# A decoder layer in split fp32: the down matrix's weight sums are made in the tail's second half instead of beside the main stage, and attention's line ends at 870

## The chip, the cores and the metric

The kernel runs on one core of one Trainium2 chip. A core has five engines with instruction streams of their own: PE (TensorE, matrix products), DVE (VectorE), ACT (ScalarE), POOL (GpSimd) and SP (SyncE, which issues most DMA transfers here). The metric is the device time of one execution in microseconds (us); the time of the kernel is the median of its runs.

## The reference

One trunk layer on 2048 tokens of 1024 channels, all in float32. It has a convolutional and an attention branch side by side, one output projection, and a gated feed-forward part of 2816 hidden channels:

```python
a = _rmsnorm(h, g_pre_mix[l])
u = jnp.einsum("bsd,dc->bsc", a, w_in[l])     # conv value | conv gate | q | k | v, 512 columns each
...
conv_out = _conformer_conv(c_val, c_gate, ...)   # GLU, causal depthwise conv of width 31, LayerNorm, silu
attn_out = _stick_breaking(q, k, v)              # 8 heads of 64; sigmoid(z) * prod of (1 - sigmoid) between
attn_out = _rmsnorm(attn_out, attn_norm_g[l]).reshape(B, S, SB_WIDTH)
y = jnp.einsum("bsc,cd->bsd", jnp.concatenate([conv_out, attn_out], axis=-1), w_out[l])
h = h + _rmsnorm(y, g_post_mix[l])
f_in = _rmsnorm(h, g_pre_ffn[l])
gt = jnp.einsum("bsd,df->bsf", f_in, w_gate[l])
up = jnp.einsum("bsd,df->bsf", f_in, w_up[l])
f = jnp.einsum("bsf,fd->bsd", jax.nn.silu(gt) * up, w_down[l])
h = h + _rmsnorm(f, g_post_ffn[l])
```

## The kernel before

**Products.** Each fp32 operand is split into a high part (`wH`, `xH`) that PE can take and a low rest (`wL`, `xL`); ACT makes the high part, POOL or DVE the rest. A product is three matrix products, low by high, high by high and high by low, on 128x512 tiles.

**The feed-forward part** uses a scheme of seven products instead of eight for each 2x2 block of matrices. It needs combinations of four quarters of the weights: per block `j` of `HF` = 11 and per matrix four sums for gate and up (88 in all, kept as `S`), and four for the down matrix (44, kept as `wd` with the numbers 5, 7, 6 and 4). `sums()` makes them on POOL from pieces of 128x512, which SP loads into three tiles called `sum`, and stores them in memory (L846 the sum, L840 the load, L768 the store).

**The main stage** walks the four groups of 512 tokens by a table, `PLAN`: the in-projection (PE writes `inps`), the two halves of the mixed output projection (`outc`, `outa`, PE writes `ops`), then products of the feed-forward part (`c11`, `p4`). The entries' costs add up to positions from 0 to 932. Beside it three generators are advanced: attention (`ATTN`), the taps of the convolution (`TAPS`, DVE, L476) and the weight sums (`SUMS`); each of the three tables says which share of its generator is due at which position. A unit of attention is: z on PE (L562, L563), sigmoids on ACT (L568, L570), a scan on DVE (`om`, L572), a product on POOL (`A`, L573), transposes on PE (`at`, L589), a split on ACT and DVE (`TH`, `TL`), and the value product `o` on PE (L594, L595). What is left of attention when the table's products are done is run alone, and then the last half of the output projection.

**The tail.** `five()` runs 44 blocks of gate and up, the first 22 for one half of the tokens and the last 22 for the other. A block is five products of twelve matrix products each (L762, PE writes `b`; four in the first half, where the fifth, `p4`, was made in the main stage). Its weights come from `S` through tiles `raw` (L1055, a DMA on SP); ACT and POOL split them (`wH` L1066, `wL` L1067). What a block adds up runs on DVE (L1074). Between the blocks a table `todo` calls other work, such as `input_sums`, which read sums of the inputs (`sumin<-B`, L815) into operands. The operands of products 6 and 5 of the first half lie in four large tiles under `x2` (`xH`, `xL`). After the first half these tiles are free until the down products, whose operands are split at L1254 to L1257 and whose products write `dps`.

**What sets the order.** Program order is a priority only: a scheduler places each engine's instructions by simulated time when the program is built. Instructions that go through `tc.keep_in_program_order` keep theirs.

Of the kernel before, what the change touches and what calls it, by code (L numbers as in the profile page):

```python
# [9 lines left out]
F32 = mybir.dt.float32  # L10
# [18 lines left out]
G = 512  # L29
# [36 lines left out]
    ("outc", 3, 22),  # L66
)

ATTN = ((46, 0.0), (890, 1.0))
TAPS = ((30, 0.0), (130, 0.168), (170, 0.25), (260, 0.418), (300, 0.5), (410, 0.668), (450, 0.75), (650, 0.918), (700, 1.0))  # L70
SUMS = ((330, 0.0), (900, 1.0))

# [66 lines left out]
def layer_kernel(ctx: ExitStack, tc: tile.TileContext, x, xT, g_pre_mix, w_in, conv_w, conv_b, ln_g, ln_b,  # L139
                 attn_g, w_out, g_post_mix, g_pre_ffn, w_gate, w_up, w_down, g_post_ffn, out):  # L140
    nc = tc.nc
# [88 lines left out]
    class Weights:  # L230
# [9 lines left out]
        def next(self):  # L240
            while len(self.tiles) < min(self.n + 1 + self.ahead, len(self.srcs)):
                self.tiles.append(self.load(self.srcs[len(self.tiles)]))
            self.n += 1
            return self.tiles[self.n - 1]
# [56 lines left out]
    for c in range(CB):  # L301
        t = vp.tile([P, PAD + G], F32, name=f"glu{c}")
# [160 lines left out]
    def taps(g):  # L463

        acc = vp.tile([P, CB, G], F32, tag="acc", name="acc", bufs=1)
        conv[g] = dp.tile([P, CB, G], F32, name=f"conv{g}")
        for c in range(CB):
            yield need(("val", g, c))
            a = pp.tile([P, G], F32, tag="cv", name="cv", bufs=1)
            tc.keep_in_program_order(  # L470
                nc.vector.tensor_scalar(a, gl[c][:, 0:G], cw[:, c, 0:1], cb_[:, c:c + 1], ALU.mult, ALU.add))
            yield 1
            for k in range(1, CW):
                to = acc[:, c, :] if k == CW - 1 else a
                tc.keep_in_program_order(
                    nc.vector.scalar_tensor_tensor(to, gl[c][:, k:k + G], cw[:, c, k:k + 1], a, ALU.mult, ALU.add))  # L476
                yield 1
            done.add(("taps", g, c))
        for _ in range(TAPLAG):
            yield 3  # L480
        yield from convnorm(g, acc)
# [265 lines left out]
    HF = NF // 2  # L747
    add, sub, mult = ALU.add, ALU.subtract, ALU.mult
# [5 lines left out]
    def four(t):  # L754
        return [t[:, i, :] for i in range(4)]
# [10 lines left out]
    def store(t, *key, eng=nc.sync):  # L766
        stored[key] = dp.tile([P, *t.shape[1:]], F32, name="_".join(str(k) for k in key))
        eng.dma_start(stored[key], t)  # L768

    def part(t, k, n, *key, eng=nc.sync):  # L770

        if key not in stored:
            stored[key] = dp.tile([P, n, G], F32, name="_".join(str(k) for k in key))
        eng.dma_start(stored[key][:, k, :], t)
# [61 lines left out]
    def sums():  # L836

        def piece(w, j, e):
            t = fup.tile([P, G], F32, tag="sum", name="sum", bufs=3)
            nc.sync.dma_start(t, w[j][:, e * G:(e + 1) * G])  # L840
            return t

        late = []

        def combine(c, a, b, op, *key):
            nc.gpsimd.tensor_tensor(c, a, b, op)  # L846
            late.append((c, *key))

        def flush(n):
            while len(late) > n:  # L850
                t, kind, *key, m = late.pop(0)
                if kind == "S":
                    ns = (6, 7) if m in (6, 7) else (5, 3)
                    part(t, ns.index(m), 2, kind, *key, ns)
                else:
                    store(t, kind, *key, m)

        for j in range(HF):
            for i, w in enumerate(W):
                a21, a22, a11 = piece(w, j + HF, 0), piece(w, j + HF, 1), piece(w, j, 0)  # L860
                yield 1
                combine(a22, a21, a22, add, "S", i, j, 5)
                yield 1
                combine(a21, a21, a11, sub, "S", i, j, 7)
                combine(a11, a22, a11, sub, "S", i, j, 6)
                yield 1
                flush(0)
                a12 = piece(w, j, 1)
                yield 1
                combine(a12, a12, a11, sub, "S", i, j, 3)  # L870
                yield 1
                flush(0)
        for j in range(HF):
            b12, b11, b22 = piece(w_down, j, 1), piece(w_down, j, 0), piece(w_down, j + HF, 1)
            yield 1
            combine(b11, b12, b11, sub, "wd", j, 5)
            yield 1
            combine(b12, b12, b22, sub, "wd", j, 7)
            combine(b22, b22, b11, sub, "wd", j, 6)
            yield 1  # L880
            flush(0)
            b21 = piece(w_down, j + HF, 0)
            yield 1
            combine(b21, b21, b22, sub, "wd", j, 4)
            yield 1
            flush(0)

    def input_sums(g, k, tmp, banks=bank, t4=None):

# [53 lines left out]
    def chain(gens):  # L943
        for gen in gens:
            yield from gen

    attn_s = Side(chain(attn(g) for g in range(NG)), 1 / (2 * NH * P * sum(16 * g + 10 for g in range(NG))), ("attn",))
    taps_s = Side(chain(taps(g) for g in range(NG)), 1 / (NG * (CB * CW + 3 * (TAPLAG + LAG * TT))), ("taps", "conv"))
    sums_s = Side(sums(), 1 / (15 * HF))
    fns = {"prep": (prep, 8), "qkv": (lambda g: inproj(g, qkv), 12), "gv": (lambda g: inproj(g, gv), 8),  # L950
           "in": (lambda g: inproj(g, both), 20),
           "mixc": (lambda g: mixed(g, 0), 1), "outc": (lambda g: outproj(g, 0), 4),
# [2 lines left out]
    def each(fn):  # L955
        def gen(g):
            for t in range(TT):
# [6 lines left out]
             "tprep": tprep}  # L964
    sides = ((attn_s, ATTN), (taps_s, TAPS), (sums_s, SUMS))
    pos = 0
    for name, g, cost, *mid in PLAN:
        fn, total = fns[name]
        pos += cost
        todo = []  # L970
# [11 lines left out]
        n = 0  # L982
# [15 lines left out]
    with ExitStack() as E:  # L998
# [6 lines left out]
        def operand(*slots, dt=F32R):  # L1005
            return [pool.tile([P, 4, G], dt, tag=tag, name=f"{tag}_", bufs=2 if pool is xp else 1)
                    for pool, tag in slots]

        e = [(ep, f"e{i}") for i in range(6)]
        x2 = [(xp, "xH"), (xp, "xL")]  # L1010
# [89 lines left out]
        late = []  # L1100

        def flush(n):
            for e in late:
                e[0] -= 1
            while n and late and late[0][0] < 0:
                store(*late.pop(0)[1:])
                n -= 1
# [4 lines left out]
        def five(early, todo):  # L1112
# [40 lines left out]
            for n in range(NB):  # L1153
                b3 = gu("b3")
                b.mul(b.b2, 7, False)
                nxt = Block(n + 1) if n + 1 < NB else None
# [41 lines left out]
                fn(*args)  # L1198
            next(more_h.pop())
            assert next(more, None) is None  # L1200
            for _ in range(9):
                flush(2)

        operands(0, [(6, x2), (5, x2), (7, e[4:6]), (3, e[0:2])])
        R = []
        last = NG - 2

        def steps():

# [18 lines left out]
        todo = {n: [(next, more)] * (1 if n < 5 else 2 - n % 2) for n in range(17)}  # L1228
        todo[17] = todo[18] = [(next, more)]
        todo[2 * HF - 1] = [(operands, last, [(3, e[0:2])], nc.gpsimd)]  # L1230
        five({2 * HF - 1: [(operands, last, [(7, e[4:6])])]}, todo)


# [164 lines left out]
```

## Time and profile before

| what | value |
|---|---|
| time, three runs | 2581.54, 2574.46, 2579.35 us; median 2579.35 |
| the profiled execution | 2579.23 us; its span 2577.5 us, mean granted clock 0.977 |
| PE | busy 2430.0 us, 94% of the span, 11156 instructions |
| POOL | busy 1482.5 us, 58% |
| DVE, ACT | busy 1793.3 us (70%), 1291.5 us (50%) |
| sums of weights, L846 | 132 of them, 171.8 us on POOL, 1302 ns each |
| the tail's two halves of gate and up | about 1557 to 1821 and 1821 to 2135 us |

The page first gives each engine's busy time. A busy engine that waits for nothing sets the pace; an idle stretch of it is what can be won. A row of waits names the engine and line that waited, the engine and line that it waited for, the total in us, how often, and the longest. In a timeline, a row gives start, duration, engine, line, operation and tiles, and in brackets the idle time before it with what ended it. In rows of the chain (the work that ended last, followed back) a row gives start, duration and what.

### The profile page before, as it was taken

What the parts mean: (1) busy time and instruction counts of PE and PEld (TensorE: products, weight loads), DVE (VectorE), ACT (ScalarE), POOL (GpSimd) and SP (SyncE); (2) the same over time, 40 slices, a digit from 0 to 9 for tenths busy, and PEclk for the clock granted to TensorE, in tenths of its full rate; (3) what the DMA queues carried; (4) which work ended last, traced back from release to release, by engine and by line L of the source; (5) the groups of instructions that cost most, each with busy time, mean ns of one, the idle gap of its engine ahead of it and who ended that gap; (6) DMA issues with size and microseconds to landing.
All of it is one profiled execution on the core that took longest, in us unless ns stands there. A gap on an engine that the chain in (4) does not pass through costs nothing.

```text
span 2577.5 us, 35682 instructions
## 1 busy us (share of the span) xinstructions
PE 2430.0 (94%) x11156; PEld 1963.3 (76%) x11156; DVE 1793.3 (70%) x2321; ACT 1291.5 (50%) x2398; POOL 1482.5 (58%) x1844
## 2 busy tenths in 40 slices
PE   7999989998999998999999979999999999998997
PEld 6878767776777776887788857777788878887886
DVE  5797689967997798887544547766655655557556
ACT  4455555655555655667666645332332233454543
POOL 5764668556755776639533228755443444567556
PEclk9999989998999899999999989999999999999999
DMA  9989877988898998857777746977656667668655
GB/s 360 303 301 311 287 244 260 369 262 272 273 328 287 314 329 285 275 189 230 263 257 243 242 140 235 340 265 234 213 189 201 199 200 266 195 189 286 204 188 171
DMA packets 289182, 657.32 MB, mean 255 GB/s; under 512 B 33888, under 2 KB 42080, under 8 KB 288992
## 3 DMA queue, kind: packets, MB, share of 16 engines
q1 hardware_dynamic: 264704, 622.01, 72.0%
q10 hardware_dynamic: 24288, 33.04, 3.5%
q8 instruction: 88, 1.44, 0.2%
q14 instruction: 102, 0.84, 0.1%
HBM read 460.92 MB, written 193.99 MB: 254 GB/s over the span
## 4 chain that ended last, share of the span: by engine, by line
PE 52%; DVE 11%; POOL 5%; DMA 4%; issue 3%; ACT 2%; SPq 0%; POOLq 0%; ACTq 0%; DVEq 0%
PE b L762 17%; PE dps L762 13%; PE c L762 8%; DVE cv L476 3%; DVE om L572 2%; PE at L589 2%; PE p L762 1%; PE ops L688 1%; PE ops L689 1%; PE ops L690 1%; PE o L595 1%; PE z L562 1%; PE o L594 1%; PE z L563 1%; DVE TL L249 1%
## 5 line engine op out<-in xcount | busy, mean ns | idle before, releaser
L573 POOL TENSOR_TENSOR A<-A,om 128x512 f32<-128x512 f32 (+2 forms) x320 | 313.7, 980 | 415.9 <-DVE om L572 364.3
L572 DVE TENSOR_TENSOR_SCAN om<-om,one,z 128x513 f32<-128x513 f32 (+2 forms) x320 | 351.3, 1112 | 114.5 <-ACT A L570 103.2
L1067 POOL TENSOR_TENSOR wL<-raw,wH 128x512 fp32r<-128x512 f32 x176 | 255.6, 1478 | 262.9 <-issue 164.6
L476 DVE SCALAR_TENSOR_TENSOR cv<-glu,cw,cv 128x512 f32<-128x512 f32 x464 | 346.6, 747 | 6.7
L1257 DVE TENSOR_TENSOR xL__22001<-t__22003,xH__22000 128x512 fp32r<-128x512 f32 x154 | 199.3, 1302 | 159.5 <-ACT xH__22000 L1256 159.3
L1255 POOL TENSOR_TENSOR xL__21999<-t__22002,xH__21998 128x512 fp32r<-128x512 f32 x154 | 207.8, 1354 | 173.3 <-ACT xH__21998 L1254 172.7
L256 PE MATMUL inps<-xH,wL 128*128 128x512 f32 x640 | 260.8, 408 | 12.9 <-ACT sg L422 11.0
L249 DVE TENSOR_TENSOR TL<-at,TH 128x512 fp32r<-128x512 f32 (+1 forms) x320 | 188.2, 598 | 110.3 <-ACT TH L248 109.8
L260 PE MATMUL inps<-xL,wH 128*128 128x512 f32 x640 | 258.4, 405 | 0.5 <-DVE xL L392 0.5
L258 PE MATMUL inps<-xH,wH 128*128 128x512 f32 x640 | 258.6, 405 | 0.0
L762 PE MATMUL dps<-xH__21998,xL__22001 128*128 128x512 f32 x616 | 240.9, 391 | 8.1 <-DVE xL__22001 L1257 7.2
L568 ACT ACTIVATE om<-z 128x512 f32<-128x512 f32 (+2 forms) x320 | 171.6, 539 | 153.0 <-DVE z L565 70.8
L762 PE MATMUL dps<-xL__21999,xH__22000 128*128 128x512 f32 x616 | 240.6, 391 | 2.2 <-POOL xL__21999 L1255 2.2
L762 PE MATMUL dps<-xH__21998,xH__22000 128*128 128x512 f32 x616 | 240.2, 390 | 0.0
L846 POOL TENSOR_TENSOR sum<-sum 128x512 f32<-128x512 f32 x132 | 171.8, 1302 | 89.3 <-DMA sum<-in_w_up_dram 33.4
L248 ACT ACTIVATE TH<-at 128x512 fp32r<-128x512 f32 (+1 forms) x320 | 168.2, 547 | 106.3 <-PE at L589 102.4
L1254 ACT ACTIVATE xH__21998<-t__22002 128x512 fp32r<-128x512 f32 x154 | 97.1, 631 | 231.9 <-POOL xL__21999 L1255 151.5
L589 PE MATMUL at<-idr,A 128*128 128x128 f32 x1088 | 192.1, 280 | 10.5 <-POOL A L573 9.3
L210 ACT ACTIVATE wH<-raw 128x1024 fp32r<-128x1024 f32 x156 | 165.8, 1065 | 53.5 <-DMA raw<-in_w_in_dram 19.1
L570 ACT ACTIVATE A<-z 128x512 f32<-128x512 f32 (+2 forms) x320 | 168.4, 542 | 21.0 <-PE at L589 13.6
L589 PEld LDWEIGHTS at<-idr,A 128*128 128x128 f32 x1088 | 142.0, 144 | 48.5 <-POOL A L573 12.4
L1066 ACT ACTIVATE wH<-raw 128x512 fp32r<-128x512 f32 x176 | 101.1, 623 | 154.8 <-PE b L762 77.1
(296 smaller groups left out, 6226.3 us busy)
## 6 DMA issues: line engine op xcount, KB each, us to landing
wL<-wL SPq DMA_DIRECT2D x156, 512.0 KB, 5.2
raw<-in_w_in_dram SPq DMA_DIRECT2D x80, 512.0 KB, 6.0
t__22003<-u SPq DMA_DIRECT2D x154, 256.0 KB, 2.8
c<-c ACTq DMA_DIRECT2D x88, 256.0 KB, 4.6
t__22002<-wd SPq DMA_DIRECT2D x88, 256.0 KB, 2.9
K<-kd SPq DMA_DIRECT2D x80, 256.0 KB, 4.6
V<-vd SPq DMA_DIRECT2D x80, 256.0 KB, 4.5
u<-accf SPq DMA_DIRECT2D x22, 768.0 KB, 4.2
```

Of the source, the lines that this page charges most:

```text
L249: nc.vector.tensor_tensor(L, ps, H.bitcast(F32), ALU.subtract)
L256: nc.tensor.matmul(ps, WL[:, kc], aH[t](k), start=k == 0, stop=False)
L258: nc.tensor.matmul(ps, WH[:, kc], aH[t](k), start=False, stop=False)
L260: nc.tensor.matmul(ps, WH[:, kc], aL[t](k), start=False, stop=k == KT - 1)
L476: nc.vector.scalar_tensor_tensor(to, gl[c][:, k:k + G], cw[:, c, k:k + 1], a, ALU.mult, ALU.add))
L572: nc.vector.tensor_tensor_scan(r, r, z[:, 0:1].to_broadcast([P, w + 1]), one, ALU.mult, ALU.bypass)
L573: nc.gpsimd.tensor_tensor(a[:, 0:w], a[:, 0:w], om[:, G - w + 1:G + 1], ALU.mult)
L589: nc.tensor.transpose(pt[:, j * P:(j + 1) * P], u["A"][j][:, b * P:(b + 1) * P], id32)
L762: return nc.tensor.matmul(ps, a, b, skip_group_check=True, **flags)
L1067: nc.gpsimd.tensor_tensor(l, t, f32(h), sub)
L1255: nc.gpsimd.tensor_tensor(WL, w, f32(WH), sub)
L1257: nc.vector.tensor_tensor(UL, t, f32(UH), sub)
```

## The change

The generator `sums()` loses the 44 sums of the down matrix, and its scale goes from 15 to 10 steps a block. A new generator `down_sums()` makes them in the tail: its pieces lie in the four tiles of `x2`, which give a ring of sixteen 128x512 pieces, four of which make up one `j`. Four pieces are loaded by SP at a time, the sums are made on POOL in place, pinned in program order, and stored through the queue `late`, from which each product of a block stores up to two entries. Blocks 22 to 43 each advance the generator twice, so two sums a block. The last flush at the end of the blocks takes twelve entries instead of nine. In the attention table, 890 becomes 870.

```diff
-ATTN = ((46, 0.0), (890, 1.0))
+ATTN = ((46, 0.0), (870, 1.0))
...
-        for j in range(HF):
-            b12, b11, b22 = piece(w_down, j, 1), piece(w_down, j, 0), piece(w_down, j + HF, 1)
-            yield 1
-            combine(b11, b12, b11, sub, "wd", j, 5)
-            yield 1
-            combine(b12, b12, b22, sub, "wd", j, 7)
-            combine(b22, b22, b11, sub, "wd", j, 6)
-            yield 1
-            flush(0)
-            b21 = piece(w_down, j + HF, 0)
-            yield 1
-            combine(b21, b21, b22, sub, "wd", j, 4)
-            yield 1
-            flush(0)
...
-    sums_s = Side(sums(), 1 / (15 * HF))
+    sums_s = Side(sums(), 1 / (10 * HF))
...
-            for _ in range(9):
+            next(more_wd)
+            for _ in range(12):
                 flush(2)
...
+        def down_sums():
+
+            wd = cycle([p for _ in range(2) for t in operand(*x2, dt=F32) for p in four(t)])
+
+            def piece(j, e, c):
+                t = next(wd)
+                nc.sync.dma_start(t, w_down[j][:, c * G:(c + 1) * G])
+                return t
+
+            def pinned(*args):
+                tc.keep_in_program_order(nc.gpsimd.tensor_tensor(*args))
+
+            def get(j):
+                return piece(j, 0, 1), piece(j, 0, 0), piece(j + HF, 0, 1), piece(j + HF, 0, 0)
+
+            nxt = get(0)
+            yield
+            for j in range(HF):
+                b12, b11, b22, b21 = nxt
+                pinned(b11, b12, b11, sub)
+                late.append([1, b11, "wd", j, 5])
+                yield
+                pinned(b12, b12, b22, sub)
+                late.append([1, b12, "wd", j, 7])
+                yield
+                pinned(b22, b22, b11, sub)
+                late.append([1, b22, "wd", j, 6])
+                yield
+                pinned(b21, b21, b22, sub)
+                late.append([1, b21, "wd", j, 4])
+                yield
+                if j + 1 < HF:
+                    nxt = get(j + 1)
...
+        more_wd = down_sums()
+        for n in range(2 * HF, 4 * HF):
+            todo[n] = todo.get(n, []) + [(next, more_wd)] * 2
```

The line numbers of the changed kernel are 14 lower between the two edits (L1067 becomes L1053, L1055 L1041), and 24 higher behind them (L1257 becomes L1281); the new load is L1201 and the new sum L1205.

Three places show how the instructions now stand. First POOL at the switch from the tail's first to its second half. `raw_19797` of before and `raw_19577` of after hold the same block's weights. Before:

```order
L1067 TENSOR_TENSOR wL<-raw_19698,wH 128x512 x2
L810 TENSOR_TENSOR e__19805<-sumin,e__19804 128x512 x4
L1067 TENSOR_TENSOR wL<-raw,wH 128x512 x2
L1067 TENSOR_TENSOR wL<-raw_19797,wH 128x512 x2
L1067 TENSOR_TENSOR wL<-raw,wH 128x512 x2
L1067 TENSOR_TENSOR wL<-raw_19924,wH 128x512 x2
```

After:

```order
L1053 TENSOR_TENSOR wL<-raw_19577,wH 128x512 x2
L1205 TENSOR_TENSOR xH__19708<-xH__19708 128x512
L1053 TENSOR_TENSOR wL<-raw,wH 128x512 x2
L1053 TENSOR_TENSOR wL<-raw_19704,wH 128x512 x2
L1205 TENSOR_TENSOR xH__19708<-xH__19708 128x512 x2
L1053 TENSOR_TENSOR wL<-raw,wH 128x512 x2
L1053 TENSOR_TENSOR wL<-raw_19808,wH 128x512 x2
L1205 TENSOR_TENSOR xH__19708<-xH__19708 128x512
L1205 TENSOR_TENSOR xL__19709<-xL__19709 128x512
```

From here to the end of the blocks, two sums (L1205) stand ahead of each block's four `wL`.

Second SP at the same switch, the queue of loads and stores. Before:

```order
L1055 DMA raw_19698<-S_0_(5, 3)_5640 128x1024
L1055 DMA raw<-S_1_(6, 7)_7123 128x1024
L1126 DMA glu_134<-c_2_1_0_0_15435 128x512
L815 DMA sumin<-B_3_18429 128x512 x4
L768 DMA u_1_10_19860<-sumf 128x512
L1051 DMA a_19793<-in_w_up_dram 128x512
L1127 DMA a_19793<-c_2_1_0_1_15532 128x512
L768 DMA u_4_10_19862<-lng 128x512
L1055 DMA raw_19797<-S_0_(5, 3)_6447 128x1024
```

After:

```order
L1041 DMA raw_19478<-S_0_(5, 3)_6136 128x1024
L1201 DMA xH__19708<-in_w_down_dram 128x512 x4
L1201 DMA xL__19709<-in_w_down_dram 128x512 x4
L1041 DMA raw<-S_1_(6, 7)_7861 128x1024
L1112 DMA glu_134<-c_2_1_0_0_15458 128x512
L815 DMA sumin<-B_3_18209 128x512
L1201 DMA xH__19710<-in_w_down_dram 128x512
L815 DMA sumin<-B_3_18209 128x512 x3
L1201 DMA xH__19710<-in_w_down_dram 128x512
L768 DMA u_1_10_19640<-sumf 128x512
L1037 DMA a_19573<-in_w_up_dram 128x512
L1113 DMA a_19573<-c_2_1_0_1_15549 128x512
```

Two more of these loads follow there ahead of the load of `raw_19577`, so twelve pieces (L1201) now stand between the load of `raw_19478` and that one, where before none did.

Third PE behind the last product of the out-projection's first half, where attention's rest is run. Before:

```order
L690 MATMUL ops_17368<-wL_17245,xH_17206 128x512
L562 MATMUL z_16877<-K_16873,QL_16280 128x512
L563 MATMUL z_16877<-K_16873,QH_16279 128x512
L594 MATMUL o_16487<-TH_16844,V_16472 128x512
L562 MATMUL z_16945<-K_16873,QL_16280 128x512
L563 MATMUL z_16945<-K_16873,QH_16279 128x512
L595 MATMUL o_16487<-TL_16845,V_16472 128x512
```

After:

```order
L690 MATMUL ops_17148<-wL_17027,xH_16988 128x512
L562 MATMUL z_16521<-K_16388,QL_15958 128x512
L563 MATMUL z_16521<-K_16388,QH_15957 128x512
L594 MATMUL o_16209<-TH_16366,V_15964 128x128
L595 MATMUL o_16209<-TL_16367,V_15964 128x128
L589 MATMUL at_16473<-idr_72,A_16203 128x128
L589 MATMUL at_16473<-idr_72,A_16257 128x128
```

Counted from here to the end of attention, before has 4 z (pairs of L562 and L563) and 9 o (pairs of L594 and L595) left on PE, after has 6 and 13.

## The prediction

> **What bounds the kernel now.** I read the page's first lines, then a table by stage, then the group, the tiles and the waits of the moved sums, then the waits before PE at the places that the new order touches. The first line of the page and its row for the sums' line:
>
> ```profile
> PE 2430.0 (94%) x11156; PEld 1963.3 (76%) x11156; DVE 1793.3 (70%) x2321; ACT 1291.5 (50%) x2398; POOL 1482.5 (58%) x1844
> L846 POOL TENSOR_TENSOR sum<-sum 128x512 f32<-128x512 f32 x132 | 171.8, 1302 | 89.3 <-DMA sum<-in_w_up_dram 33.4
> ```
>
> PE works 2430.0 of 2577.5 us, so 147.5 us of PE's idle time and whatever the clock loses are all that a change without matrix products can touch. Next the table of stretches (busy us of PE, PEld, DVE, ACT, POOL; granted clock; DMA share; GB/s), and the same table for the sums' line alone:
>
> ```profile
> 660.00:1050.00 390.00, 359.82 (x1754) 289.53 (x1753) 341.81 (x472) 222.93 (x417) 266.64 (x388) 0.98 0.89 305
> 825.00:850.00 25.00, 20.75 (x104) 17.07 (x104) 12.68 (x21) 13.35 (x28) 11.70 (x21) 0.93 0.87 293
> 875.00:900.00 25.00, 20.20 (x92) 15.62 (x93) 24.12 (x38) 16.66 (x35) 15.15 (x30) 0.80 1.04 390
> 1494.00:1527.00 33.00, 19.01 (x67) 13.46 (x66) 16.09 (x22) 15.75 (x29) 7.98 (x14) 0.68 0.42 143
> 1800.00:1835.00 35.00, 29.80 (x126) 23.11 (x126) 25.74 (x30) 13.85 (x25) 22.46 (x16) 1.00 0.63 219
> 1831.00:2115.00 284.00, 283.18 (x1215) 228.92 (x1216) 163.53 (x202) 80.75 (x141) 119.31 (x84) 1.00 0.59 193
> ...
> 660.00:1050.00 390.00, 57.19 (x44) 0.98 0.89 305
> ```
>
> The 44 sums of the down matrix's weights all lie in 660 to 1050, a stretch in which PE idles 390 − 359.82 = 30.2 us and the DMA engines are at 0.89. The tail's second half, 1831 to 2115, is the opposite: PE idles 0.8 us, POOL works 119.31 of 284 and the DMA engines are at 0.59. So the change takes work out of a stretch with holes and puts it into one that PE fills.
>
> **The change, part by part.** First what the main stage is freed of: the stores of the sums, the waits of POOL and of SP's queue on them, and the one place where they reach PE, in the order of time (start, duration, in brackets the idle time before and its releaser):
>
> ```profile
> L768 SPq DMA_DIRECT2D wd<-sum x44: 319/382/1381, 664.4 to 1045.4; - x44
> ...
> SPq L840 <- DMA wd<-sum: 21.5, 13, 4.9
> SPq L768 <- POOL sum L846: 16.0, 10, 3.6
> ...
> POOL sum L846 <- DMA sum<-in_w_down_dram: 8.1, 5, 4.3
> ...
> 831.42 1.27 POOL L846 TENSOR_TENSOR sum<-sum 128x512 f32<-128x512 f32 x1 [4.29 <-DMA sum<-in_w_down_dram]
> 834.60 0.75 DVE L498 SCALAR_TENSOR_TENSOR cy<-cy,mv,lnb 128x512 f32<-128x512 f32 x1 [3.96 <-POOL mv L192]
> 835.38 0.63 ACT L500 ACTIVATE cs<-cy 128x512 f32<-128x512 f32 x1 [4.12 <-DVE cy L498]
> 836.83 0.73 PE L256 MATMUL inps<-xH,wL 128*128 128x512 f32 x1 [4.25 <-ACT sg L422]
> ```
>
> (a) The chain at 831 reads: a load for a sum is late, POOL stands 4.29 us before the sum, the layer norm's `mv` waits behind it on POOL, DVE 3.96 us for `mv`, ACT 4.12 for DVE, PE 4.25 us for ACT. Without the sum this goes: 4.25 us, and the clock of 0.93 in those 25 us, 0.07 × 25 = 1.75 us more, makes −6.0. The other 30.2 − 4.25 = 25.9 us of idle time in 660 to 1050 have other names:
>
> ```profile
> PE z L562 <- DVE om L572: 13.9, 16, 1.6
> PE inps L256 <- ACT sg L422: 6.2, 2, 4.2
> ...
> L476 DVE SCALAR_TENSOR_TENSOR cv<-glu,cw,cv x464: 722/747/757, 30.6 to 1127.4; 128x512 f32<-128x512 f32 x155
> ```
>
> The largest is PE's wait for the attention scan on DVE, which is 341.81 of 390 busy with its own work; the conv taps, the most frequent work there, take 722 to 757 ns whatever POOL does, so POOL's 57.19 us less don't shorten them. But SP was blocked 21.5 + 16.0 = 37.5 us by the sums' stores and tile slots, with all other loads and stores of the main stage queued behind, and 44 loads and 44 stores of 256 KB leave a stretch in which DMA is near full. I let 3 of the 25.9 us go: −9 in all. Bounds: −4 (the wait of 4.25 alone) and −19 (6.0, and half of 25.9). The gate and up sums stand at the same places of POOL's queue in both orders, so the new scale of their line is 0.
>
> (b) Attention's line now ends at 870 instead of 890. By the order, attention ends later all the same: behind the last product of the out-projection's first half, 4 z and 9 o units were left, now 6 z and 13 o units. Those run alone. PE there, and the price of a unit's four transposes where PE is full, from the chain:
>
> ```profile
> 1494.04 0.40 PE L690 MATMUL ops<-wL,xH 128*128 128x512 f32 x1
> 1494.27 0.39 PE L562 MATMUL z<-K,QL 128*128 128x512 f32 x1
> 1494.50 0.39 PE L563 MATMUL z<-K,QH 128*128 128x512 f32 x1
> ...
> 1500.26 0.80 PE L562 MATMUL z<-K,QL 128*128 128x512 f32 x1 [3.80 <-DVE om L572]
> ...
> 1516.65 0.50 PE L595 MATMUL o<-TL,V 128*128 128x512 f32 x1
> ...
> 1523.54 1.09 PE L627 MATMUL po<-idr,ot 128*128 128x128 f32 x4 [5.04 <-DVE ot L619]
> 1526.65 0.79 PE L688 MATMUL ops<-wH,e__17289 128*128 128x512 f32 x1 [2.02 <-DVE e__17289 L527]
> ...
> 846.62 0.44 PE at L589 x4
> ```
>
> Nine units from 1494.27 to 1517.15 are 22.9 / 9 = 2.54 us each, since each waits for DVE, ACT and POOL in turn and the clock is 0.68. Where PE is full a unit is four products 0.23 us apart and the transposes, 4 × 0.23 + 0.44 = 1.36 us. Four more units here and four fewer there: 4 × (2.54 − 1.36) = +5. Bounds: 0 (a longer queue overlaps better) and +10 (4 × 2.54: what the full stage is spared, it idles away). The norm behind the last unit (the 5.04 and 2.02 us) stays.
>
> (c) The loads of the first 12 pieces stand on SP at the switch to the second half, ahead of the load of weight sums on which PE waits there today:
>
> ```profile
> 1817.84 2.77 DMA sumin<-B
> ...
> 1821.93 5.71 DMA raw<-S_(5, 3)_6447
> ...
> 1830.05 1.72 POOL wL L1067
> ...
> PE b L762 <- POOL wL L1067: 4.3, 3, 3.0
> ```
>
> Twelve pieces of 128 × 512 × 4 bytes are 3.15 MB; at the 390 GB/s of 875 to 900, the fastest row above, that is 8.1 us if the load stands behind all of them, and nothing if they fit into what 219 GB/s in 1800 to 1835 leaves free. Part of them is issued a block earlier, and PE's wait of 3.0 is there already: I take +2, bounds 0 and +8.
>
> (d) The second half itself. POOL gets 57.19 us: 119.3 + 57.2 = 176.5 of 284. Two sums a block, 2.6 us, stand in POOL's queue ahead of four `wL` of a block:
>
> ```profile
> 1939.13 6.41 POOL L1067 TENSOR_TENSOR wL<-raw,wH 128x512 fp32r<-128x512 f32 x4 [8.64 <-issue]
> 1953.40 5.04 POOL L1067 TENSOR_TENSOR wL<-raw,wH 128x512 fp32r<-128x512 f32 x4 [7.86 <-issue]
> ```
>
> POOL idles 7.9 to 8.6 us ahead of each such group, so the sums run in that gap, and their pieces are loaded eight blocks ahead, so POOL has nothing to wait for. DMA gets 44 loads and 44 stores, 23 MB in 284 us or 81 GB/s on 193, and a share of 0.59 × 274 / 193 = 0.84, under the 0.89 that the main stage ran with. SP gets 88 issues of 383 ns (the row of the stores above), 34 us of 284; a store goes out a product after its sum, so that the loads queued behind it don't wait for POOL. So 0. Bounds: −0.8 (all the idle time there is) and +3 (one wait as long as the 3.0 above). Without the gaps the 44 sums would be 57 us.
>
> (e) The end of the second half, where POOL and DVE start on the down products while PE still has products of blocks:
>
> ```profile
> 2124.43 2.85 DVE L1257 TENSOR_TENSOR xL__22001<-t__22003,xH__22000 128x512 fp32r<-128x512 f32 x2
> ...
> 2127.94 0.73 PE L762 MATMUL b<-e__18328,a22h 128*128 128x512 f32 x2 [2.28 <-DVE glu L1074]
> ```
>
> PE waits 2.28 us behind two early L1257 on DVE. Their slots now hold pieces until the last sums are stored, so the splits start later and DVE is free for `glu`; but the first down product's operand also comes later. I take −1, bounds −2.3 (the wait) and +4 (twice the pair's 2.85 less that wait, rounded up).
>
> Sum: −9 + 5 + 2 + 0 − 1 = −3. The profiled execution took 2579.23 us, 0.1 under the median of 2579.35, so both give 2576.
>
> **The rivals.** R1, the main stage gains what its queue lost: SP's 37.5 us of blocking hides behind several names (the loads behind the 25.9 us), and the relief is near its bound of −19. For it speaks the DMA share of 1.04 with a clock of 0.80 in 875 to 900; against it that DVE, not a DMA, is named in PE's largest wait. −19 + 5 = −14: 2565.
>
> R2, on the other side, attention's end: if the whole of 1494 to 1527 grows with the units, 33 × 13 / 9 = 47.7, that is +14.7, and with the least relief of −4 it is +10.7: 2590. It decides from a growth of 12 us (4 + 7.7). For it: the clock of 0.68 there, which longer idling won't lift; against it: the last 10 us of the 33 are the norm, once, whatever the count.
>
> R3, the ports of DVE and POOL in the second half. DVE's additions there, and its split of the down operands next to POOL's:
>
> ```profile
> L1074 DVE TENSOR_TENSOR a22h<-a,a22h x22: 679/682/686, 1821.2 to 2115.1; 128x512 fp32r<-128x512 f32 x22
> L1074 DVE TENSOR_TENSOR sumf<-a,sumf x21: 677/685/1778, 1582.5 to 2098.3; 128x512 f32<-128x512 f32 x21
> L1257 DVE TENSOR_TENSOR xL__22001<-t__22003,xH__22000 x154: 677/1361/1784, 2120.1 to 2557.7; 128x512 fp32r<-128x512 f32 x154
> ```
>
> The split takes 1361 ns in the median where POOL works beside it, 677 at best; an addition took 1778 once. If all 22 + 21 were stretched by 1778 − 685 = 1.09 us and PE waited for each, 47 us: 2623. The Trainium skill (SBUF — State Buffer, Who interferes with whom) has a rule for it: a DVE instruction with two SBUF inputs and a GpSimd instruction that reads SBUF exclude each other for the whole instruction. By that rule the main stage's taps at L476 should have been stretched by the sums too, and 757 ns at most says that they weren't; the split at L1257 agrees. Against R3: DVE idles 284 − 163.53 = 120 us there, so a stretched addition has room. It decides from a sixth of them on PE's path.
>
> R4, nothing happens: the sums were not in the way, the scheduler fills their place with other waits of the same chain, and the second half hides them: 2579.
>
> **How the numbers follow.** About 0.3% (7.7 us) is what a measurement of this kernel can tell from no change. The forecast has 0.35, R4 0.10, both within it: 0.45 same. R1 0.33 faster. R2 0.17 and R3 0.05 slower: 0.22. The point is the forecast's, 2576. The range reaches to R1 and a little past it, since (a) is bounded by −19 and (e) by −2.3: 2562; above to R2 at 2590, rounded to 2591. Outside are R3 and the sums of all bounds (−22 and +21), 2 in 10. The forecast's own range is 2571.6 to 2587.
>
> **What would show it.** (a) right: no wait of PE near 830, and PE's idle time in the stretch that held the sums down from 30 to about 21 us; wrong if it stays at 28 or more. (b) right: attention's end lasts about 38 us. (c) right: PE's waits on `wL` at the switch are 3 to 6 us; wrong at 8 or more. (d) right: PE idles under 3 us in the second half, sums of 1.3 us between the `wL`, and DVE's `sumf` still near 685 ns; R3 shows there. (e) PE's wait of 2.28 us for `glu` is gone. The forecast is wrong above all if the 25.9 us move by more than 10, which the waits of before do not tell.

## The result and the profile after

The changed kernel takes 2567.52 us (median of 8 runs, 2556.38 to 2571.49); the kernel before, on the same chip beside it, 2581.34 us (8 runs). The ratio is 0.9942, 95% interval 0.9928 to 0.9956: 13.8 us faster by the medians. The profiled execution's span is 2565.7 us, 11.8 under that of before. The page's first line of the changed kernel, and its table of stretches (columns as before; its second row is attention's end, then come the switch, the tail's second half and its end):

```profile
PE 2430.8 (95%) x11156; PEld 1959.6 (76%) x11156; DVE 1800.1 (70%) x2321; ACT 1290.6 (50%) x2398; POOL 1493.5 (58%) x1844
...
660.00:1050.00 390.00, 371.81 (x1832) 300.68 (x1831) 337.69 (x475) 229.04 (x422) 214.03 (x341) 1.00 0.77 258
...
1475.00:1514.00 39.00, 24.30 (x95) 15.99 (x93) 22.01 (x29) 19.71 (x37) 11.49 (x19) 0.81 0.35 124
...
1753.80:1833.80 80.00, 77.19 (x329) 61.37 (x328) 54.04 (x62) 27.39 (x49) 45.95 (x31) 1.00 0.83 287
...
1835.00:2115.00 280.00, 280.00 (x1203) 226.31 (x1203) 176.45 (x202) 80.59 (x141) 179.37 (x124) 1.00 0.76 261
...
2115.00:2125.00 10.00, 10.00 (x46) 8.17 (x45) 9.61 (x13) 3.64 (x7) 2.63 (x2) 1.00 0.95 322
```

PE works as long as before (2430.8 us). In 660 to 1050 its idle time falls from 30.2 to 18.2 us and the granted clock goes from 0.98 to 1.00. In the second half PE has no idle time at all, though POOL's work there rose from 119 us of 284 to 179 of 280.

Three rows of PE's timeline cut the execution into the same pieces in every kernel: the last product of the out-projection's first half (L690 with xH), the first of its second half (which reads `e__`), and the first down product (`dps`). After, and the one row of before that isn't shown above:

```profile
1475.49 0.39 PE L690 MATMUL ops<-wL,xH 128*128 128x512 f32 x1
...
1513.85 0.79 PE L688 MATMUL ops<-wH,e__17069 128*128 128x512 f32 x1 [2.02 <-DVE e__17069 L527]
...
2119.53 0.39 PE L762 MATMUL dps<-xH__21958,xL__21961 128*128 128x512 f32 x1
...
2133.62 0.40 PE L762 MATMUL dps<-xH__21998,xL__22001 128*128 128x512 f32 x1
```

| piece | before | after | difference |
|---|---|---|---|
| main stage, to the last L690 with xH | 1494.04 | 1475.49 | −18.5 |
| attention's end, to the first `e__` product | 32.6 | 38.4 | +5.8 |
| tail, to the first `dps` | 607.0 | 605.7 | −1.3 |
| down products, to the end of the span | 443.9 | 446.2 | +2.3 |

Four units that the main stage no longer runs are 4 × 1.36 = 5.4 us of its 18.5, by the prediction's price. What is left, 13.1 us, is the gain of the main stage, and 5.8 − 5.4 = 0.4 the cost at attention's end. Some 5 us of the 13.1 arise between 385 and 434 us, before the first sum of the down matrix: there PE waits 3.5 us for a `wL` of the out-projection before, and 0.4 after. The last experiment, whose main stage is that of the kernel before, has 2.6 us of that wait and still ends its main stage 3.5 us earlier, so a difference of a few us between two single executions is not shown to be the change's. The 2.3 us of the down products are of that kind: 446.1 in the last experiment too. The medians carry the total; the pieces say where.

The main stage's waits in 660 to 1050, PE's of the changed kernel:

```profile
PE z L562 <- DVE om L572: 5.0, 8, 0.8
...
PE inps L256 <- ACT sg L422: 0.8, 2, 0.5
```

They were 13.9 and 6.2 us. The wait for the scan fell by 8.9; the prediction had put it down to DVE's own work. With 850 it is 5.4, and with the sums moved and the line at 890 it is 8.3.

### The profile page after: what moved, and what is told of

The parts are those of the page before. It is cut to its first block, busy times and chain, and to the rows that moved or that the text cites. A ratio compares the mean times of both kernels' runs of the same rounds, so it can differ in the third digit from the quotient of the medians.

```text
span 2565.7 us, 35691 instructions
## 1 busy us (share of the span) xinstructions
PE 2430.8 (95%) x11156; PEld 1959.6 (76%) x11156; DVE 1800.1 (70%) x2321; ACT 1290.6 (50%) x2398; POOL 1493.5 (58%) x1844
## 5 line engine op out<-in xcount | busy, mean ns | idle before, releaser
L1053 POOL TENSOR_TENSOR wL<-raw,wH 128x512 fp32r<-128x512 f32 x176 | 253.3, 1464 | 204.3 <-ACT wH L1052 194.7
L476 DVE SCALAR_TENSOR_TENSOR cv<-glu,cw,cv 128x512 f32<-128x512 f32 x464 | 346.8, 747 | 6.7
L1281 DVE TENSOR_TENSOR xL__21961<-t__21963,xH__21960 128x512 fp32r<-128x512 f32 x154 | 196.0, 1282 | 156.1 <-ACT xH__21960 L1280 156.0
L570 ACT ACTIVATE A<-z 128x512 f32<-128x512 f32 (+2 forms) x320 | 167.8, 539 | 12.3 <-PE at L589 11.9
L846 POOL TENSOR_TENSOR sum<-sum 128x512 f32<-128x512 f32 x88 | 115.4, 1312 | 79.4 <-DMA sum<-in_w_up_dram 41.6
```

The lines of the kernel that those rows point to most:

```text
L1053: nc.gpsimd.tensor_tensor(l, t, f32(h), sub)
L1281: nc.vector.tensor_tensor(UL, t, f32(UH), sub)
```

## The experiments

All ratios are to the kernel before, run beside them on the same chip; the changed kernel's is 0.9942.

| kernel | line | left at attention's end | ratio, 95% interval | last L690 | end | tail |
|---|---|---|---|---|---|---|
| before | 890 | 9 | 1 | 1494.0 | 32.6 | 607.0 |
| line alone | 870 | 13 | 1.0067, 1.0046 to 1.0089 | 1504.2 | 37.6 | 612.7 |
| sums moved alone | 890 | 24 | 0.9993, 0.9978 to 1.0008 | 1463.2 | 61.9 | 605.4 |
| changed | 870 | 13 | 0.9942, 0.9928 to 0.9956 | 1475.5 | 38.4 | 605.7 |
| changed, 850 | 850 | 8 | 0.9942, 0.9925 to 0.9960 | 1491.2 | 26.9 | 603.9 |
| changed, 800 | 800 | 0 | 0.9939, 0.9917 to 0.9960 | 1504.3 | 11.4 | 601.8 |
| no sums in the tail | 870 | 13 | 0.9951, 0.9931 to 0.9970 | 1478.4 | 37.4 | 610.6 |
| no additions | 870 | 13 | 0.9963, 0.9947 to 0.9979 | 1481.6 | 35.9 | 608.1 |
| additions only | 850 | 13 | 1.0003, 0.9990 to 1.0017 | 1489.2 | 37.3 | 613.3 |
| sums doubled in the tail | 870 | 13 | 0.9961, 0.9949 to 0.9974 | 1476.2 | 38.8 | 616.4 |
| changed, pinned | 870 | 4 | 0.9972, 0.9957 to 0.9987 | 1506.2 | 17.0 | 605.4 |
| changed, pinned, later table | 870 | 8 | 1.0025, 1.0011 to 1.0039 | 1486.0 | 31.1 | 619.9 |
| before, pinned | 890 | 0 | 1.0071, 1.0055 to 1.0087 | 1521.2 | 13.6 | 618.0 |
| before, four additions on DVE | 890 | 9 | 0.9965, 0.9947 to 0.9984 | 1490.5 | 31.2 | 605.2 |

**The two halves of the change.** First the line alone, an edit of before:

```diff
-ATTN = ((46, 0.0), (890, 1.0))
+ATTN = ((46, 0.0), (870, 1.0))
```

> The kernel before with only its attention table changed, 890 to 870; the down matrix's sums stay in the main stage. By the order 6 z and 13 o units are left behind the out-projection's first half, as in the changed kernel. Theory A (the main stage gains because the sums are gone from it): no gain here, 2578 to 2588 against 2581 before, with the sums' stall chain still there. Rival B (the gain comes from attention's line and the new order it brings): 2565 to 2573, most of the change's 14 us.

2599.05 us, ratio 1.0067: neither theory had that; the line alone costs 17.6 us. POOL's waits in 600 to 1050 in this kernel, and the table for that stretch, then the same row of the changed kernel:

```profile
POOL sum L846 <- DMA sum<-in_w_down_dram: 30.4, 10, 7.6
...
POOL sum L846 <- DMA sum<-in_w_up_dram: 18.7, 4, 6.1
...
600.00:1050.00 450.00, 408.39 (x1892) 323.05 (x1891) 368.85 (x513) 247.23 (x463) 291.55 (x418) 0.94 0.85 291
```

```profile
600.00:1050.00 450.00, 420.64 (x2024) 336.19 (x2023) 388.49 (x546) 263.95 (x490) 249.04 (x398) 0.97 0.76 255
```

Attention stands in both at the same places to within two units (by the order, 144 units lie ahead of the in-projection's 1680th product in both), so the difference is the sums'. With them POOL stands 30.4 us for their loads, against 8.1 us in the kernel before, and PE does 1892 instead of 2024 instructions in the stretch, at a clock of 0.94 instead of 0.97. So the line is no gain of its own, and rival B falls.

The other half is the changed kernel with the line put back to 890:

> The changed kernel with attention's line ending at 890 as before: the sums are moved, the line is not. By the order 17 z and 24 o units are left at attention's end, 11 more than with 870. With the prediction's price of 2.54 - 1.36 = 1.18 us a unit that is 13 us more than the changed kernel: 2580. With the price that the two traces show (the end grew by 6.6 us for 4 units, 1.65 each, less 1.36 spared before) it is 0.3 us a unit: 2571. Rival B: the gain hangs on the line, so it is gone, 2580 or more, but with the main stage up to attention's end no earlier than before.

2580.49 us, ratio 0.9993: as predicted by the larger price in time, but not in its place. The main stage is earlier by 12.3 us than with 870, and attention's end longer by 23.6:

```profile
1463.23 0.40 PE L690 MATMUL ops<-wL,xH 128*128 128x512 f32 x1
...
1525.15 0.79 PE L688 MATMUL ops<-wH,e__17069 128*128 128x512 f32 x1 [2.02 <-DVE e__17069 L527]
```

Neither half gains; together they gain 0.6%. The sums' move frees the main stage, in which the scheduler then runs fewer units of attention beside the same products, 24 being left at the end; the line draws 11 of them back, which the freed main stage can take and the one with the sums cannot.

**How far the line should go.** The changed kernel with 800 and with 850:

> The changed kernel with attention's line ending at 800: by the order no z and no o unit is left behind the out-projection's first half. With 1.18 us a unit, 13 units make -15: 2552. With 0.3 us a unit: -4, 2563. Rival C: attention's units, drawn forward, crowd DVE in the stretch where it is at 0.88, and the main stage gives back what the end gains: 2566 to 2575.

> The changed kernel with attention's line ending at 850: by the order 1 z and 8 o units are left at attention's end instead of 6 and 13. Beside 890 (24 left, 2580), 870 (13 left, 2567.5) and 800 (none left, 2566) it shows whether there is a best place between. By the two traces a unit fewer at the end is worth 0.8 to 0.9 us, and units drawn forward cost the stretch around 600 to 660 about that from 870 to 800: 2563 if the loss there begins late, 2567 if it is even, 2570 or more if the loss begins at once.

2565.71 us (0.9939) and 2569.97 us beside a slower before (0.9942): both as fast as with 870. With 800 the two rows of the end are:

```profile
1504.30 0.39 PE L690 MATMUL ops<-wL,xH 128*128 128x512 f32 x1
...
1515.72 0.80 PE L688 MATMUL ops<-wH,e__17069 128*128 128x512 f32 x1 [2.02 <-DVE e__17069 L527]
```

Without a unit left the end is 11.4 us, the norm. With 8, 9, 13 and 24 units it is 26.9, 32.6, 38.4 and 61.9, all within 2.5 us of 11.4 + 2.1 a unit. But the main stage gives it back: from 870 to 800 thirteen units more cost it 28.8 us, 2.2 each. From 890 to 870 eleven units cost it 12.3, 1.1 each: that is the step that pays. So the prediction's 1.36 us for a unit in the main stage is near the price of that step and too low below 870. There the main stage gives back what the end gains, as rival C said; that DVE is what the units crowd there, as it also said, is not shown.

**What the tail pays for the sums.** The changed kernel without them:

```diff
-            next(more_wd)
...
-            for n in range(2 * HF, 4 * HF):
-                todo[n] = todo.get(n, []) + [(next, more_wd)] * 2
...
-                nc.sync.dma_start(w, stored["wd", j, n])
+                nc.sync.dma_start(w, w_down[j + HF * (n < 6)][:, 0:G])
```

> The changed kernel without the down matrix's sums at all: the new generator is not called, and the down products read a plain piece of the matrix where they read a sum. It prices the 44 sums, 44 loads and 44 stores of the tail's second half. If they are hidden, as the prediction has it: within 3 us of the changed kernel, 2565 to 2568. If the switch's loads, the ports of DVE and POOL or the end of the half cost something: 2562 or less, with the difference at that place.

2568.64 us, ratio 0.9951: the 44 sums cost nothing that can be measured; in the profile the tail without them is even 4.9 us longer (610.6). Some 3 of these are a wait at the switch that before has too and the changed kernel has not; the section on the switch shows its cause:

```profile
PE b L762 <- POOL wL L1053: 4.4, 3, 3.0
```

Then twice the additions:

```diff
                 tc.keep_in_program_order(nc.gpsimd.tensor_tensor(*args))
+                tc.keep_in_program_order(nc.gpsimd.tensor_tensor(args[0], args[0], args[0], add))
```

> The changed kernel with a second addition on POOL behind each of the 44 sums in the tail's second half (the piece added to itself, which changes its value). It tests the cover: POOL worked 179 of 280 us there, and 44 more of 1.68 us are 74, so 253. If the sums run in POOL's gaps, PE still has no wait there: 2565 to 2571. If the gaps are smaller than they look, a block's weights come late: PE waits on the weights' low parts in the second half, 2575 or more, up to 2567 + 74.

2573.82 us, ratio 0.9961 (0.9949 to 0.9974): some 5 us over the changed kernel, with intervals that still overlap, and not where the second theory put it. The second half, then the first down product and what it waits for:

```profile
1840.00:2115.00 275.00, 275.00 (x1182) 222.28 (x1181) 178.63 (x197) 79.22 (x138) 222.40 (x164) 1.00 0.79 264
...
ACT xH__22004 L1281 <- DMA wd<-xH__19710: 16.1, 1, 16.1
...
2131.33 0.80 PE L762 MATMUL dps<-xH__22002,xL__22005 128*128 128x512 f32 x1 [11.35 <-DVE xL__22005 L1282]
```

With POOL at 222 of 275 us PE still does not wait in the blocks. In this execution (2580.97 us, above the median) it waits 11.35 us once, at the first down product: its operand goes into a slot from which the last sums are still being stored. That is the prediction's step (e), with its loss instead of its gain.

**Additions or traffic.** Two kernels split what the sums do to the main stage. The first stores the loaded pieces as they are, the second makes the additions from tiles that are there already:

```diff
-            combine(b11, b12, b11, sub, "wd", j, 5)
+            late.append((b11, "wd", j, 5))
```

> The kernel before with attention's line at 870 (2599 in the run of the line alone), and POOL's 44 additions for the down matrix left out: its 44 loads and 44 stores stay in the main stage, and the loaded pieces are stored as they are. Attention's place is that of the changed kernel to within two units, with 13 units left at its end. If POOL's part is what hurts the main stage (its time, or its standing still for a late load with others queued behind): 2565 to 2575, the changed kernel's time. If it is the traffic and SP's queue: 2590 to 2600. In between, both.

```diff
-            b12, b11, b22 = piece(w_down, j, 1), piece(w_down, j, 0), piece(w_down, j + HF, 1)
+            b12, b11, b22 = (fup.tile([P, G], F32, tag="sum", name="sum", bufs=3) for _ in range(3))
...
-            combine(b11, b12, b11, sub, "wd", j, 5)
+            nc.gpsimd.tensor_tensor(b11, lng, lnb, sub)
```

> The other half: POOL's 44 additions stay in the main stage, but on tiles that are there already, with no load and no store of the down matrix's pieces; the down products read plain pieces. Attention's line is at 850, because with that the order leaves 6 z and 13 o units at its end and stands within three units of the changed kernel on the way. If POOL's time of 57 us itself hurts: 2585 to 2600. If it is the traffic and SP's queue, or POOL's standing still for late loads: 2565 to 2575. If this one and the one without additions are both near the changed kernel, it is the addition that waits for its load, and neither alone.

Without additions: 2575.60 us, ratio 0.9963, that is 27 us under the line alone and 5 us over the changed kernel. With additions only: 2583.64 us, ratio 1.0003, 16 us over the changed kernel with the same line (850), just under the first theory's range. Both lack the tail's sums and so have a longer tail (608.1 and 613.3), and the line alone has one too (612.7). What the main stage pays is therefore better read at the first `e__` product, where the tail begins. Against the changed kernel with the same line it comes 3.7 us later without additions (1517.50 and 1513.85), 8.5 later with additions only (1526.53 and 1518.05), and 27.9 later with both, in the line alone (1541.79 and 1513.85). By subtraction, some 16 of the 28 us come only where both are together, each addition waiting for its own load and each store for its addition; POOL stood 30.4 us for these loads in the line alone. POOL's time by itself comes second and the traffic last. These sizes are rough: they are single executions, the order shifts with each edit, and the additions without loads do not lie where the others do (from 657 to 760 us, in the line alone from 657 to 947), since nothing holds them back.

PE's wait for the scan in 660 to 1050 goes the same way. The line alone, then the kernel without additions, with two of SP's waits in 600 to 1050:

```profile
PE z L562 <- DVE om L572: 11.8, 12, 3.0
```

```profile
PE z L562 <- DVE om L572: 5.8, 9, 2.6
...
SPq L768 <- DMA sum<-in_w_down_dram: 30.3, 20, 3.7
...
SPq L840 <- DMA wd<-sum: 8.3, 17, 1.1
```

With additions only it is 8.0 us, and 5.4 in the changed kernel with the same line. SP's queue stands 38.6 us for the pieces' loads and stores in the kernel without additions, as long as the 37.5 that rival R1 counted, and the main stage still has nearly the whole gain.

**Another place in the main stage.** Without pinning, the scheduler makes the sums well ahead of their table: the first of the changed kernel's 88 starts at 18 us, the last at 651. Pinned, they follow it: the first starts at 384, the second at 589 and the last at 1505. The edit is one line, in the changed kernel, then with a later table, then in the kernel before:

```diff
-            nc.gpsimd.tensor_tensor(c, a, b, op)
+            tc.keep_in_program_order(nc.gpsimd.tensor_tensor(c, a, b, op))
```

> The changed kernel with the 88 sums for gate and up pinned in program order on POOL. Unpinned, the scheduler places them ahead of attention's 122nd unit (until 651 us) whatever their table says; pinned, the table (330 to 900) places them from the 74th unit to the last, so most fall in 600 to 1480. At attention's end no z and 4 o units are left instead of 6 and 13. If sums cost time because of the stretch they lie in (short of time on DVE and POOL, not PE), the time goes where they go: the stretch up to 600, whose PE idles, gets shorter, and 600 to 1050 longer: 2555 to 2570. If POOL's time costs nothing in itself and the order is what matters: no forecast better than 2567 plus or minus 8.

> The same with the sums' table from 560 to 900: they lie from attention's 212th unit to its end, that is in the stretch from about 1050 on, where PE is busy for 0.98 of the time and POOL for 0.47. 2 z and 8 o units are left. If additions on POOL hurt only where PE waits for the attention chain: all stretches before 1050 are freed of 88 sums, 115 us of POOL and 46 MB of traffic, and the late one hides them: 2535 to 2555. If they hurt anywhere in the main stage: no faster than the changed kernel, or slower where attention's end now has to wait for the sums: 2565 to 2585.

> The kernel before, with attention's line at 890 and all 132 sums in the main stage, but pinned on POOL, so that its table (330 to 900) spreads them from attention's 71st unit to the last; the down matrix's 44 then lie behind the 248th unit, beyond 1150. If it is the place of the sums and not their being in the main stage: as fast as the changed kernel or faster, 2550 to 2568. If they cost the same at any place of the main stage: 2578 or more.

2573.05 us (0.9972, 0.9957 to 0.9987), 2588.65 us (1.0025, 1.0011 to 1.0039) and 2599.59 us (1.0071, 1.0055 to 1.0087). All three are slower than the changed kernel, and the first theory of each, 2555 to 2570, 2535 to 2555 and 2550 to 2568, missed. In the second of them, the end of the last in-projection and the stretch in which the sums now lie, then the same two rows of the changed kernel:

```profile
864.73 0.40 PE L260 MATMUL inps<-xL,wH 128*128 128x512 f32 x1
...
1050.00:1480.00 430.00, 410.96 (x1981) 330.42 (x1980) 263.88 (x336) 276.12 (x511) 273.65 (x423) 0.98 0.88 302
```

```profile
878.88 0.39 PE L260 MATMUL inps<-xL,wH 128*128 128x512 f32 x1
...
1050.00:1480.00 430.00, 422.32 (x2086) 344.57 (x2084) 275.33 (x360) 289.81 (x542) 206.00 (x379) 1.00 0.71 236
```

Freed of 88 sums, the stages up to the last in-projection are 14.2 us shorter. But the stretch in which PE seemed full takes them no better: PE loses 11.4 us of 430 and some of the clock, and at the first `e__` product the 14.2 us are gone (1517.12, against 1513.85, or 1518.05 with the line at 850, which leaves the same 8 units). So up to there a sum costs about as much late as early. What makes this kernel 21 us slower than the changed one lies mostly behind: its last sum starts at 1579 us, in the tail's first blocks, and its tail is 14.2 us longer. The pinned kernel before is alike, with its last sum at 1573 us, 8.1 us of loss up to the first `e__` product and a tail 11.0 us longer. In the first of the three, whose sums end at 1505, the loss of 9.3 us lies ahead of the tail, which is as long as the changed kernel's. By what the late sums hold up the tail was not tried. Of the places tried, only the tail's second half, which has no attention beside it, hides the sums.

**The switch.** Before, PE waits 3.02 us there for `wL`. POOL before, then after:

```profile
1823.72 6.37 POOL L810 TENSOR_TENSOR e__19805<-sumin,e__19804 128x512 fp32r<-128x512 f32 x4 [4.77 <-ACT e__19804 L809]
1830.05 5.45 POOL L1067 TENSOR_TENSOR wL<-raw,wH 128x512 fp32r<-128x512 f32 x4
```

```profile
1815.46 1.29 POOL L810 TENSOR_TENSOR e__19585<-sumin,e__19584 128x512 fp32r<-128x512 f32 x1 [4.77 <-ACT e__19584 L809]
1816.71 3.44 POOL L1053 TENSOR_TENSOR wL<-raw,wH 128x512 fp32r<-128x512 f32 x2
1820.12 4.70 POOL L810 TENSOR_TENSOR e__19585<-sumin,e__19584 128x512 fp32r<-128x512 f32 x3
```

Before, all four additions for the last operand stand ahead of the block's `wL`; after, two `wL` have come between the first and the others. This was in the order that the document shows above, and was overlooked. The last experiment takes the additions off POOL in the kernel before:

```diff
-        todo[2 * HF - 1] = [(operands, last, [(3, e[0:2])], nc.gpsimd)]
+        todo[2 * HF - 1] = [(operands, last, [(3, e[0:2])])]
```

> The kernel before with one word changed in the tail: the four additions that make the last operand at the switch to the second half run on DVE instead of POOL, so no four additions of 6.4 us stand ahead of the next block's weights on POOL; the loads and their order are as before. If PE's wait of 3.0 us for the weights' low part there came from POOL's order: it is gone, the tail from the output projection's second half to the first down product is 603 to 605 us instead of 607.0, and the time 2576 to 2581. If it came from the late load of the weight sums, as the prediction has it: the wait is still 2.5 us or more, and nothing is faster.

2573.71 us, ratio 0.9965 (0.9947 to 0.9984). PE's waits on `wL` in the tail, here and in the changed kernel (4.3, 3 times, longest 3.0, before):

```profile
PE b L762 <- POOL wL L1067: 1.2, 2, 1.0
```

```profile
PE b L762 <- POOL wL L1053: 1.5, 2, 1.0
```

The wait is gone with the loads left as they are, and the tail is 605.2 us: it was POOL's order. So some 3 of the change's 13.8 us come from how its pinned sums reorder POOL at the switch, and moving four additions to DVE wins them without any sum moved. The ratio's 9 us are more than these 3 explain; in its profile the main stage, untouched, is 3.5 us earlier too, and what the rest is stays open.

## Why the prediction was right or wrong

The time, 2567.5, lies within the range, but below the forecast's own part of it, 2571.6 to 2587, and near rival R1's 2565; the forecast of 2576 had the sign, and a quarter of the size. The range held because it reached down to R1, and R1's reason did not hold: that part is luck. In the profiles the terms add up to −13.1 + 0.4 for the main stage and attention's end, −1.3 for the tail, and +2.3 for the down products, for which the prediction had no term: −11.7 in all.

- **(a)** was −9 and came out as −13.1, within its bounds, of which some 5 may be another execution's and not the change's. The chain at 831 is gone as said. Mis-sized was the term for the other 25.9 us of PE's idle time: it was 3, and they fell by 7.7, to 18.2. I read a wait for DVE's scan as DVE's own. The additions stand in that chain: leaving them out, with loads, stores and the line kept, takes the wait from 11.8 to 5.8 us. R1 was the right size for the wrong reason: it named SP's queue, which stands as long without the additions and costs little, and the traffic is the smallest of the three parts. By which buffer or queue POOL's sums reach the scan was not tried.
- **(b)** was +5 net and came out as +0.4. The end of about 38 us agrees with 38.4 by luck: with the prediction's own 2.54 us a unit, four units make it 32.6 + 10.2 = 43. That price had shared out the pipeline's start over nine units; each further one costs 1.4 to 2.1. And I compared 9 with 13 units, the change with before, but never asked what each half leaves: the line is what keeps 24 from being left.
- **(c)** was +2 and was wrong in sign and cause: the wait of 3.02 us is gone. The whole tail is only 1.3 us shorter, since PE's waits for `lnb` (2.5 to 4.3) and `cs` (0.6 to 2.0) grew, for which there was no term and no cause is shown. The chain showed the load of `raw` ahead of the wait, and I priced loads; the last link in front of PE was POOL, working off additions.
- **(d)** was right: 0, and the cover is wide, since in the blocks twice the additions don't break it. R3's mechanism is there:

```profile
L1060 DVE TENSOR_TENSOR sumf<-a,sumf x21: 676/903/1853, 1570.9 to 2086.8; 128x512 f32<-128x512 f32 x21
L1060 DVE TENSOR_TENSOR sumf<-b,sumf x16: 683/691/692, 1573.0 to 2121.8; 128x512 f32<-128x512 f32 x16
...
L1205 POOL TENSOR_TENSOR xH__19708<-xH__19708 x12: 1287/1299/1748, 1827.7 to 2074.3; 128x512 f32<-128x512 f32 x12
L1205 POOL TENSOR_TENSOR xL__19709<-xL__19709 x12: 1289/1680/1850, 1852.8 to 2101.7; 128x512 f32<-128x512 f32 x12
```

  DVE's additions of the first row go from 685 to 903 ns in the median. On three of the four tiles the sums have a median of 1680 ns and take up to 1850, and 1299 on the first, where the main stage's had 1292. Not every row of DVE grows (`accf<-sumf,accf` goes from 1772 to 683), but DVE's work in 1835 to 2115 rises from 163 to 176 us, and PE waits for none of it. The Trainium skill's rule (SBUF — State Buffer, Who interferes with whom) agrees with these rows; it says who is slowed, not whether anyone waits. The additions of the second row read `b`, which lies in PSUM, the memory that PE writes; they have only one input in SBUF, the other on-chip memory, and stay at 692 ns at most. The same settles the taps at L476, which the prediction held against the rule: their `cv` is a tile of the PSUM pool `pp`, so they too have one tile in SBUF, and their 757 ns at most fit it.
- **(e)** was −1; the wait of 2.28 us is gone, and PE has no idle time from 2115 to 2125 (the last row of the first table). The doubled additions show the other side of it, 11.35 us.
- **R2** needed the end to grow by 12 us, and it grew by 5.8: the norm in it is a fixed 11.4 us, as the prediction's own objection said. **R4**, that nothing happens, is excluded by the interval, 0.9928 to 0.9956; the sums were in the way.

## What to carry to other kernels

Filler work on an engine that a dependent chain passes through is not free because that engine idles, and not even where PE looks full: beside attention a sum cost some 0.2 us as an addition alone and some 0.6 us with a load of its own and a store (8.5 and 27.9 us for 44), and nothing in a stretch where the engine only prepares weights one block ahead. Most of the price came where the addition had to wait for its load, so look at that wait before the addition's own time. When work is moved out of a scheduled stage, set the neighbour's progress line anew and test both halves apart: each of them alone gained nothing or lost 0.7%, and only the pair gained. And before a wait is put down to a transfer, read what the engine named in the wait did in the microseconds before it.

## What was not expected of the hardware

An addition of 128x512 on POOL takes 1.29 us in the median beside DVE's work on the main stage; in the tail's second half, it is 1.68 us on three of the four tiles, beside additions on DVE. Those of them with both inputs in SBUF took up to 1.85 us, those with one input in PSUM 0.70 at most. And two executions whose PE order is the same up to attention's end (before and the last experiment) differ by 3.5 us at the last L690 with xH, as much as several terms of the sum; terms of that size can only be read from a named wait, not from a difference of two spans.
